# Modulation's vector products in runs of four weight units, most of them moved into the second block's first layer

## The chip, the cores and the metric

One core of one Trainium2 chip. The metric is the device time of one execution in microseconds (us), the median over several executions. One execution was also taken by the hardware profiler, and all rows below come from that one.

## What is computed

Two blocks of two layers each work on 256 tokens of width 1024. The second block's layers also carry 256 context tokens in layer 0, so that their matrix products have 512 token columns there. What the change touches is the modulation of the second block: three vectors for each of two conditions, from one vector of 1024 times a matrix of 1024 x 3072.

```
def hybrid_layer_2(xs, cs, c, c_ctx, norm_g, w_mod, b_mod, w_in, b_in, ...):
    shift_x, scale_x, gate_x = jnp.split(jax.nn.silu(c) @ w_mod + b_mod, 3, axis=-1)
    shift_c, scale_c, gate_c = jnp.split(jax.nn.silu(c_ctx) @ w_mod + b_mod, 3, axis=-1)
    hx = rms_norm(xs, norm_g) * (1 + scale_x[:, None]) + shift_x[:, None]
    hc = rms_norm(cs, norm_g) * (1 + scale_c) + shift_c
    px = split_cols(hx @ w_in + b_in)
    ...
    xs = xs + gate_x[:, None] * merge(px, ya_x, yb_x, yc_x)
    ...

def reference(...):
    x = first_block(x, w_in, b_f, ...)          # two attention layers
    return second_block(x, c_2, ctx_2, ...)     # two of hybrid_layer_2
```

## The kernel before

All weights pass through one stream, `WStream`. A weight unit is 128 partitions x 1024 floats (512 KB) in most cases. `_dma` (L113 to L123) issues its load on the SP queue into a buffer of the tag `wraw`; there are four of these (`RAW` in `KN`). `_split` (L125 to L136) turns it into two single-pass operands, `wh` by a cast on ACT (L133) and `wl` by a subtraction on DVE (L134), in rings of five buffers (`WB`). When both are done, the `wraw` buffer is free for the next load. The table of units has one order, and loads are issued on SP in that order, each waiting there until its buffer is free. `ahead(i)` (L147) keeps the program's loads six units and its splits three units ahead of unit i.

A product with a split unit is three matmuls for each piece (L163, L164, L165: high x high, low x high, high x low). In the second block's layer 0 a unit's 24 matmuls have 512 columns; in the first block a unit has 12 of them.

The modulation is 48 units, 24 for each layer of the second block. Names: `1mod00` is layer 1, vector 0, eighth 0 of the contraction; vector 1 is the scale, 0 the shift, 2 the gate, and `MORDER` puts them as 1, 0, 2. Such a unit isn't split: `whole` (L138) hands out the raw float buffer, and PE reads it directly in four matmuls of 256 columns, each with a 32-wide stationary operand in its own quarter of the array (L749). A float matmul is two PE instructions in the trace, so that a unit is eight instructions. Its `wraw` buffer is free when its four matmuls are through.

Where the 48 units stand is set by `FILL`: a list of a weight unit's name and a number. `get(key)` of that unit first draws so many modulation units from the generator `mod_stream` (L740), and the table of loads has them directly ahead of that unit. `1B2 2` puts two units ahead of `1B2`, the third unit of product B in the first block's layer 1. In the names, `1A` to `1I` and `1O` are the first block's layer 1; `0AKV`, `0AQ`, `0BQ`, `0Va`, `0Vb`, `0GK`, `0GQ`, `0GV`, `0ag`, `0m3_`, `0oa` are the second block's layer 0, in this order; `1GK`, `1GV`, `1ag` are its layer 1. The scale and the shift of layer 0 are needed by the second block's first normalization, its gate only at that layer's end, and layer 1's at the next normalization. The order in which an engine runs its instructions is fixed when the program is built, by priorities that follow the order in which the code is written.

Of the kernel before, what the change touches and what calls it, by code (L numbers as in the profile page):

```python
# [38 lines left out]

MORDER = (1, 0, 2)  # L40

FILL = '1B2 2 1E2 3 1D2 3 1F0 2 1G0 2 1H2 1 0Va0 2 0Va1 2 0Va2 2 0GV0 1 0ag0 2 0ag2 2 1GV0 3 1ag0 2 1ag2 2 1A0 1 0BQ2 2 1F2 2 1GK0 1 1B0 1 1A3 5 1C2 1 0ag1 1 1H0 1 0GK0 2'

# [55 lines left out]
class WStream:  # L101
# [50 lines left out]

    def get(self, key):
        self.ad, self.asp = self.looks.pop(key, (self.ad, self.asp))
        for _ in range(self.fills.pop(key, 0)):
            next(self.stream)
        i = self.idx[key]
        self.ahead(i)
        return self.spl[i]
# [581 lines left out]
def mod_stream(g, l, W):  # L741

    nc, sp, pp = g.nc, g.sp, g.pp
    for s in MORDER:
        ps = pp.tile([128, 256], F32, name=f'mod{l}{s}', tag='gm', bufs=g.GM)
        for k in range(8):
            w = W.whole(f'{l}mod{s}{k}')
            for q in range(4):
                nc.tensor.matmul(ps[32 * q:32 * q + 32], g.cz[:, k // 2, 2 * (k % 2):2 * (k % 2) + 32],  # L749
                                 w[:, 0, 256 * q:256 * q + 256], start=k == 0, stop=k == 7)  # L750
            if k < 7:
                yield
        r = sp.tile([128, 256], F32, name=f'modr{l}{s}', tag='tg', bufs=TG)
        nc.scalar.copy(r, ps)
        pt = pp.tile([128, 2, 4, 2], F32, name=f'modt{l}{s}', tag='at', bufs=g.AT)
        for i in range(2):
            nc.tensor.matmul(pt[:, i].rearrange("p q w -> p (q w)"), r[:, 128 * i:128 * i + 128], g.sel8,
                             start=True, stop=True)
        ks = slice(8 * s, 8 * s + 8)
        v = lambda t: t.rearrange("p (q i) w -> p q i w", q=4)  # L760
        nc.vector.tensor_add(v(g.mod[l][:, ks, :]), pt.rearrange("p i q w -> p q i w"),
                             v(g.bmod[l][:, ks, None].to_broadcast([128, 8, 2])))
        if s == 1:

            nc.vector.scalar_tensor_tensor(g.modA[l], g.mod[l][:, ks, :], 1.0,
                                           g.ng[l][:, :, None].to_broadcast([128, 8, 2]), op0=OP.add, op1=OP.mult)
        yield
# [915 lines left out]
def program(ctx, tc, ins, out, parts=(1, 2)):  # L1683
# [3 lines left out]
    f32 = {e[0] for e in mods}  # L1687
    fs = FILL.split()
    fills = {k: int(n) for k, n in zip(fs[::2], fs[1::2])}
# [19 lines left out]
    looks = {k: (int(a), int(b)) for k, a, b in zip(ls[::3], ls[1::3], ls[2::3])}  # L1709
    W = WStream(g, tab, looks, f32, fills)  # L1710
    W.stream = itertools.chain(mod_stream(g, 0, W), mod_stream(g, 1, W))

    xsp = g.dram.tile([128, 2048], F32, name='xsp')
# [80 lines left out]
```

## Time and profile before

| what | value |
|---|---|
| median of 3 runs | 1210.46 us (1206.68 to 1213.55) |
| profiled execution, its own time | 1205.08 us |
| its span, first to last instruction | 1203.3 us |
| mean granted clock of TensorE | 0.996 |
| busy: PE, DVE, ACT | 1179.3, 919.3, 571.3 us |
| instructions on L749 (modulation) | 384 PE matmul instructions, 48 units |

Engines: PE is TensorE's matmul, PEld its weight load, DVE VectorE, ACT ScalarE, SP the engine on whose queue the loads are issued (SPq). Busy time of PE is modelled from the starts of pipelined matmuls, so a busy PE can still lose time between them; the distance of two starts says more than the duration. Times in rows are microseconds from the span's start.

### The profile page before, as it was taken

To read this page: it belongs to the slowest core of one execution; us is meant where nothing else is said; L and a number is where in the kernel's file an instruction comes from. 1 tells how busy PE (TensorE), PEld (TensorE's weight loads), DVE (VectorE), ACT (ScalarE), POOL (GpSimd) and SP (SyncE) were. 2 spreads that over 40 slices of the span, in tenths; PEclk is the share of its full clock that TensorE was granted. 3 is DMA by queue.
4 is the path that set the end of the run, shared out by engine and by line. 5 is a ranking of instruction groups with operands and counts; after the bars stand their busy time and mean duration, and the time that the engine had idled before them with its cause. 6 is when DMAs were issued, how large, how long until landed. Compare 5 with 4: busy or idle time off the path is not lost.

```text
span 1203.3 us, 20615 instructions
## 1 busy us (share of the span) xinstructions
PE 1179.3 (98%) x8012; PEld 980.5 (81%) x8012; DVE 919.3 (76%) x2050; ACT 571.3 (47%) x1024; POOL 11.2 (1%) x42
## 2 busy tenths in 40 slices
PE   8999999999999999999899999999999999999998
PEld 6878767677887777777788888888999768999998
DVE  5996766966799769989955535755799887896984
ACT  5556534466565433246354522433455433855552
POOL 0000000000000000000000000000000000000000
PEclk9999999999999999999999999999999999999999
DMA  7734566565555632141032232324545323653552
GB/s 249 227 122 135 184 200 233 162 219 198 187 188 207 197 135 73 43 133 54 19 124 70 88 98 78 105 90 173 176 141 189 108 89 101 198 159 123 176 176 71
DMA packets 48258, 171.33 MB, mean 142 GB/s; under 512 B 5340, under 2 KB 6492, under 8 KB 47392
## 3 DMA queue, kind: packets, MB, share of 16 engines
q1 hardware_dynamic: 48160, 170.01, 43.5%
q8 instruction: 63, 1.03, 0.4%
q14 instruction: 35, 0.29, 0.1%
HBM read 167.89 MB, written 2.10 MB: 141 GB/s over the span
## 4 chain that ended last, share of the span: by engine, by line
PE 75%; DVE 14%; DMA 4%; ACT 4%; issue 2%; SPq 0%; ACTq 0%; DVEq 0%
PE f0m L163 3%; PE f0m L165 3%; PE f0m L164 3%; PE f1m L165 2%; PE f1m L163 2%; PE f1m L164 2%; PE mod L749 1%; PE po L164 1%; PE po L165 1%; PE po L163 1%; PE go L165 1%; PE go L164 1%; PE go L163 1%; PE yog L165 1%; PE yoc L165 1%
## 5 line engine op out<-in xcount | busy, mean ns | idle before, releaser
L991 DVE SCALAR_TENSOR_TENSOR ucv<-up,par,ucv 128x512 f32<-128x512 f32 (+1 forms) x240 | 146.9, 612 | 2.2
L163 PE MATMUL f0m<-hTh,wh_0m 128*128 128x512 f32 x192 | 75.7, 394 | 0.0
L164 PE MATMUL f0m<-hTl,wh_0m 128*128 128x512 f32 x192 | 75.4, 393 | 0.0
L165 PE MATMUL f0m<-hTh,wl_0m 128*128 128x512 f32 x192 | 75.2, 392 | 0.0
L163 PE MATMUL f1m<-hTh,wh_1m 128*128 128x256 f32 x192 | 54.9, 286 | 0.1
L165 PE MATMUL f1m<-hTh,wl_1m 128*128 128x256 f32 x192 | 54.8, 286 | 0.0
L164 PE MATMUL f1m<-hTl,wh_1m 128*128 128x256 f32 x192 | 54.5, 284 | 0.0
L134 DVE TENSOR_TENSOR wl_0m<-wr_0m,wh_0m 128x1024 fp32r<-128x1024 f32 x24 | 29.3, 1221 | 25.5 <-ACT wh_0m L133 25.5
L133 ACT CAST wh_0m<-wr_0m 128x1024 fp32r<-128x1024 f32 x24 | 25.2, 1051 | 43.8 <-PE f0m L164 15.2
L163 PEld LDWEIGHTS f0m<-hTh,wh_0m 128*128 128x128 f32 x192 | 36.3, 189 | 7.7 <-DVE wl_0m L134 0.3
L164 PEld LDWEIGHTS f0m<-hTl,wh_0m 128*128 128x128 f32 x192 | 36.1, 188 | 7.5 <-issue 0.2
L165 PEld LDWEIGHTS f0m<-hTh,wl_0m 128*128 128x128 f32 x192 | 36.2, 189 | 7.3
L163 PEld LDWEIGHTS f1m<-hTh,wh_1m 128*128 128x128 f32 x192 | 36.8, 192 | 0.5 <-ACT wh_1m L133 0.3
L165 PEld LDWEIGHTS f1m<-hTh,wl_1m 128*128 128x128 f32 x192 | 36.7, 191 | 0.2 <-DVE wl_1m L134 0.2
L164 PEld LDWEIGHTS f1m<-hTl,wh_1m 128*128 128x128 f32 x192 | 36.7, 191 | 0.1
L133 ACT CAST wh_1m<-wr_1m 128x1024 fp32r<-128x1024 f32 x24 | 25.0, 1049 | 24.4 <-PE f1m L164 9.9
L134 DVE TENSOR_TENSOR wl_1m<-wr_1m,wh_1m 128x1024 fp32r<-128x1024 f32 x24 | 29.3, 1220 | 8.6 <-ACT wh_1m L133 8.4
L1271 ACT ACTIVATE mtm<-f0m,hbin 128x512 f32<-128x512 f32 x24 | 16.3, 681 | 7.6 <-DVE acc L1284 7.3
L134 DVE TENSOR_TENSOR wl_0o<-wr_0o,wh_0o 128x1024 fp32r<-128x1024 f32 x8 | 9.8, 1224 | 13.2 <-ACT wh_0o L133 13.2
L1385 DVE SCALAR_TENSOR_TENSOR xT<-po,mod,xT 128x256 f32<-128x256 f32 x16 | 7.7, 483 | 14.6 <-PE po L165 14.6
L164 PE MATMUL po<-mgl,wh_0o 128*128 128x256 f32 x64 | 18.2, 285 | 0.0
L164 PE MATMUL pp<-mgl,wh_0p 128*128 128x256 f32 x64 | 18.2, 284 | 0.0
(1854 smaller groups left out, 3979.8 us busy)
## 6 DMA issues: line engine op xcount, KB each, us to landing
wr_0mod<-in_wm_dram SPq DMA_DIRECT2D x24, 512.0 KB, 4.3
wr_1mod<-in_wm_dram SPq DMA_DIRECT2D x24, 512.0 KB, 3.7
wr_0m<-in_w_dram SPq DMA_DIRECT2D x24, 512.0 KB, 3.5
wr_1m<-in_w_dram SPq DMA_DIRECT2D x24, 512.0 KB, 3.5
wr_0O<-in_w1o_dram SPq DMA_DIRECT2D x8, 512.0 KB, 3.6
wr_1O<-in_w1o_dram SPq DMA_DIRECT2D x8, 512.0 KB, 3.5
wr_0o<-in_wo_dram SPq DMA_DIRECT2D x8, 512.0 KB, 3.5
wr_0p<-in_wo_dram SPq DMA_DIRECT2D x8, 512.0 KB, 4.3
```

The lines of the kernel that those rows point to most:

```text
L133: g.nc.scalar.copy(wh, r)
L134: g.nc.vector.tensor_sub(wl, r, wh.bitcast(F32))
L163: nc.tensor.matmul(out, lh, rh, start=start, stop=False)
L164: nc.tensor.matmul(out, lh, rl, start=False, stop=False)
L165: nc.tensor.matmul(out, ll, rh, start=False, stop=stop)
L749: nc.tensor.matmul(ps[32 * q:32 * q + 32], g.cz[:, k // 2, 2 * (k % 2):2 * (k % 2) + 32], w[:, 0, 256 * q:256 * q + 256], start=k == 0, st ...
L991: yield nc.vector.scalar_tensor_tensor(o, src, dw[:, i, j:j + 1], o, op0=OP.mult, op1=OP.add)
L1271: nc.scalar.activation(sg, pm, AF.Tanh, scale=0.5, bias=hb[:, blk(n, f)])
L1385: nc.vector.scalar_tensor_tensor(r[:, f, :], ps[:, :256], g.mod[l][:, 16 + f, w:w + 1], r[:, f, :], op0=OP.mult, op1=OP.add)
```

## The change

`FILL` is another list. Of the 48 modulation units, 24 stood in the first block's layer 1, 16 in the second block's layer 0 and 8 in its layer 1; now 16 stand in the first block's layer 1 (as 1, 5, 1, 2, 3 and 4) and 32 in the second block's layer 0 (eight times 4). `get` now cuts a number into runs of at most four units. At the first unit of a run of more than one, `mod_stream` issues the loads of the whole run, and the run's first matmul waits for the last load of the run as well.

```
-FILL = '1B2 2 1E2 3 1D2 3 1F0 2 1G0 2 1H2 1 0Va0 2 0Va1 2 0Va2 2 0GV0 1 0ag0 2 0ag2 2 1GV0 3 1ag0 2 1ag2 2 1A0 1 0BQ2 2 1F2 2 1GK0 1 1B0 1 1A3 5 1C2 1 0ag1 1 1H0 1 0GK0 2'
+FILL = '1A0 1 1A3 5 1B0 1 1B2 2 1E2 3 1D2 4 0Va0 4 0Va1 4 0Va3 4 0GK0 4 0GV0 4 0ag0 4 0ag3 4 0m3_2 4'
...
-        for _ in range(self.fills.pop(key, 0)):
+        n = self.fills.pop(key, 0)
+        for j in range(n):
+
+            self.go = min(4, n - j) if j % 4 == 0 else 0
             next(self.stream)
...
+            i = W.idx[f'{l}mod{s}{k}']
+            if W.go > 1:
+                W.ahead(i + W.go - 1)
+                last = W.loads[W.table[i + W.go - 1][0]]
             w = W.whole(f'{l}mod{s}{k}')
             for q in range(4):
-                nc.tensor.matmul(ps[32 * q:32 * q + 32], g.cz[:, k // 2, 2 * (k % 2):2 * (k % 2) + 32],
+                m = nc.tensor.matmul(ps[32 * q:32 * q + 32], g.cz[:, k // 2, 2 * (k % 2):2 * (k % 2) + 32],
                                  w[:, 0, 256 * q:256 * q + 256], start=k == 0, stop=k == 7)
+                if W.go > 1 and q == 0:
+                    g.wait(m, last)
```

PE, second block, from the last product of `0BQ` to the first of `0Va0`. Before (`t0BQ` and `f0Va` are the products' accumulators, `wh`/`wl` the split weights, `wr_1mod12` a raw modulation unit):

```order
L163 MATMUL t0BQ3_4149<-wh_0BQ3_4173,hTh1_0_3339 128x512
L749 MATMUL mod11_4170<-wr_1mod12_4150,cz_1338 32x256 x4
L749 MATMUL mod11_4170<-wr_1mod13_4158,cz_1338 32x256 x4
L163 MATMUL f0Va0_4303<-hTh0_0_3338,wh_0Va0_4197 128x512
L164 MATMUL f0Va0_4303<-hTl0_0_3340,wh_0Va0_4197 128x512
L164 MATMUL t0BQ2_4148<-wl_0BQ3_4174,hTh1_0_3339 128x512
```

The same place in the change:

```order
L168 MATMUL t0BQ3_4098<-wh_0BQ3_4101,hTl1_0_3286 128x512
L756 MATMUL mod02_4213<-wr_0mod20_3887,cz_1338 32x256
L940 MATMUL akt02_4027<-cst_66,kb2_0_3995 128x128
L926 MATMUL lrt03_4062<-cst_66,kb3_0_4058 96x128
L756 MATMUL mod02_4213<-wr_0mod20_3887,cz_1338 32x256 x3
L756 MATMUL mod02_4213<-wr_0mod21_3899,cz_1338 32x256 x4
L756 MATMUL mod02_4213<-wr_0mod22_4099,cz_1338 32x256 x4
L756 MATMUL mod02_4213<-wr_0mod23_4111,cz_1338 32x256 x4
L940 MATMUL akt03_4090<-cst_66,kb3_0_4058 128x128
L166 MATMUL f0Va0_4248<-hTh0_0_3283,wh_0Va0_4222 128x512
L167 MATMUL f0Va0_4248<-hTl0_0_3285,wh_0Va0_4222 128x512
L166 MATMUL f0Vb0_4275<-hTh0_0_3283,wh_0Vb0_4226 128x512
```

Two units in a run have become four, and `0BQ3`'s remaining products, which stood behind the run, now stand ahead of it.

SP, the loads around the same place, with the semaphores that each waits for. Before:

```order
L120 DMA wr_1mod12_4150<-in_wm_1_dram 128x1024 [waits DMAHW0_49,PE_49]
L120 DMA wr_1mod13_4158<-in_wm_1_dram 128x1024 [waits DMAHW1_49,PE_49]
L120 DMA wr_0Va0_4171<-in_w2_0_dram 128x1024 [waits DMAHW3_49,DVE_49]
L120 DMA wr_0Vb0_4181<-in_w2_0_dram 128x1024 [waits DMAHW5_49,PE_49]
L120 DMA wr_1mod14_4187<-in_wm_1_dram 128x1024 [waits DMAHW6_49,PE_49]
```

In the change:

```order
L120 DMA wr_0mod20_3887<-in_wm_0_dram 128x1024 [waits DMAHW3_49,DMAHW6_49,DVE_49,Activation_49]
L120 DMA wr_0mod21_3899<-in_wm_0_dram 128x1024 [waits DMAHW7_49,DMAHW4_49,DVE_49]
L120 DMA wr_0mod22_4099<-in_wm_0_dram 128x1024 [waits DMAHW0_49,DVE_49]
L120 DMA wr_0mod23_4111<-in_wm_0_dram 128x1024 [waits DMAHW1_49,DVE_49,Activation_49]
L871 DMA gvb_0_3696<-in_rowp_dram 128x512 [waits DVE_49]
L120 DMA wr_0Va0_4119<-in_w2_0_dram 128x1024 [waits DMAHW3_49,PE_49]
L120 DMA wr_0Vb0_4127<-in_w2_0_dram 128x1024 [waits DMAHW4_49,PE_49]
```

`0Va0`'s load waited for a split on DVE and now waits for PE; with four units in a row in the table, the four buffers ahead of it are all the run's own.

PE, the run ahead of `0ag3`, in the change alone (before, no unit stood here):

```order
L756 MATMUL mod12_5814<-wr_1mod23_5712,cz_1338 32x256 x4
L166 MATMUL f0ag3_5857<-hTh0_0_3283,wh_0ag3_5823 128x512
L167 MATMUL f0ag3_5857<-hTl0_0_3285,wh_0ag3_5823 128x512
L166 MATMUL f0m3_0_5891<-hTh0_0_3283,wh_0m3_0_5827 128x512
L167 MATMUL f0m3_0_5891<-hTl0_0_3285,wh_0m3_0_5827 128x512
L166 MATMUL f0m3_1_5920<-hTh0_0_3283,wh_0m3_1_5831 128x512
L168 MATMUL f0ag3_5857<-hTh0_0_3283,wl_0ag3_5824 128x512
```

Behind the run come at once the first products of three units that stand behind it in the table of loads.

## Rows read from the trace of the kernel before

**Rows 1.** The page: the span; PE's busy time, share and instructions.

```profile
span 1203.3 us, 20615 instructions
PE 1179.3 (98%) x8012; PEld 980.5 (81%) x8012; DVE 919.3 (76%) x2050; ACT 571.3 (47%) x1024; POOL 11.2 (1%) x42
```

**Rows 2.** Waits of PE over the span (total us, times, longest).

```profile
PE mod L749 <- DMA wr_0mod<-in_wm_dram: 1.1, 1, 1.1
PE f0Va L163 <- ACT wh_0Va L133: 0.8, 1, 0.8
```

**Rows 3.** Timeline of PE, first modulation runs (start, us, engine, line, op, out<-in, count).

```profile
163.21 0.62 PE L749 MATMUL mod<-wr_0mod,cz 128*32 128x256 f32 x4
...
165.08 0.66 PE L636 MATMUL yt<-cst,mx 128*128 128x128 f32 x4
165.49 0.46 PE L163 MATMUL g1A<-wh_1A,xTh 128*128 128x460 f32 x1
165.78 0.37 PE L164 MATMUL g1A<-wl_1A,xTh 128*128 128x460 f32 x1
166.09 0.64 PE L749 MATMUL mod<-wr_0mod,cz 128*32 128x256 f32 x8
166.66 0.48 PE L165 MATMUL g1A<-wh_1A,xTl 128*128 128x460 f32 x1
166.97 0.37 PE L163 MATMUL g1A<-wh_1A,xTh 128*128 128x460 f32 x1
167.18 0.37 PE L164 MATMUL g1A<-wl_1A,xTh 128*128 128x460 f32 x1
```

**Rows 4.** Timeline of PE, last modulation run of the kernel.

```profile
1016.65 0.28 PE L164 MATMUL f1ag<-hTl,wh_1ag 128*128 128x256 f32 x1
1016.77 0.28 PE L165 MATMUL f1ag<-hTh,wl_1ag 128*128 128x256 f32 x1
1016.98 1.07 PE L749 MATMUL mod<-wr_1mod,cz 128*32 128x256 f32 x16
1017.98 0.39 PE L163 MATMUL f1ag<-hTh,wh_1ag 128*128 128x256 f32 x1
1018.20 0.28 PE L164 MATMUL f1ag<-hTl,wh_1ag 128*128 128x256 f32 x1
```

**Rows 5.** Timeline of PE around the run of three units ahead of `1E2`, and `1E3`.

```profile
202.69 0.39 PE L164 MATMUL g1E<-wl_1E,xTh 128*128 128x512 f32 x1
202.92 0.39 PE L165 MATMUL g1E<-wh_1E,xTl 128*128 128x512 f32 x1
203.24 1.50 PE L749 MATMUL mod<-wr_0mod,cz 128*32 128x256 f32 x24
204.67 0.50 PE L163 MATMUL g1E<-wh_1E,xTh 128*128 128x512 f32 x1
...
208.62 0.73 PE L163 MATMUL g1E<-wh_1E,xTh 128*128 128x512 f32 x2
...
209.93 0.50 PE L164 MATMUL g1E<-wl_1E,xTh 128*128 128x512 f32 x1
```

**Rows 6.** Timeline of SP's queue: the issue of `1E3`'s load.

```profile
203.94 0.33 SPq L120 DMA_DIRECT2D wr_1E<-in_w_dram  x1
```

**Rows 7.** Timeline of ACT: the cast of `1E3`, with ACT's idle time before it.

```profile
207.53 1.05 ACT L133 CAST wh_1E<-wr_1E 128x1024 fp32r<-128x1024 f32 x1 [3.64 <-DMA wr_1E<-in_w_dram]
```

**Rows 8.** Timeline of ACT: casts of two loads that landed one behind the other.

```profile
408.11 1.05 ACT L133 CAST wh_0Vb<-wr_0Vb 128x1024 fp32r<-128x1024 f32 x1 [1.95 <-DMA wr_0Vb<-in_w_dram]
409.49 1.05 ACT L133 CAST wh_0Va<-wr_0Va 128x1024 fp32r<-128x1024 f32 x1 [0.33 <-DMA wr_0Va<-in_w_dram]
```

**Rows 9.** The four loads of tile `wr_0Va`, from issue to landing.

```profile
DMA to landing us min/median/max: 4.4/5.0/5.5
```

**Rows 10.** Busy time by stretch: us, PE, PEld, DVE, ACT, POOL, PEclk, DMA share, GB/s.

```profile
596.00:600.40 4.40, 2.10 (x39) 1.57 (x38) 4.40 (x11) 0.00 (x0) 0.17 (x2) 1.00 0.00 0
600.40:607.20 6.80, 6.80 (x42) 5.92 (x40) 6.80 (x9) 0.69 (x1) 0.00 (x0) 0.52 0.49 134
```

## The prediction

> **What bounds the kernel now.** I read the page first, then the timeline of PE around L749, then the queues of the loads. The page gives PE 1179.3 of the span's 1203.3 us [rows 1]: there is no stage in which another engine has the time to spare that PE lacks, so what counts is how far apart PE's matmuls start. The list of PE's waits shows how little it stands still for weights in the steady part: its longest wait for a load is 1.1 us in one place, and 0.8 us in one place for a cast [rows 2]. So the change can win only what PE pays for the modulation itself, and it can lose whatever it opens between PE's matmuls.
>
> **What a run costs.** The timeline shows 36 separate runs of L749, from 163.21 to 1016.98 [rows 3, 4]. Around the run of 8 instructions the matmul before starts at 165.78 and the second one after at 166.97; without the run these two steps would take 0.21 each (166.97 to 167.18), so the run costs 1.19 - 0.42 = 0.77 us [rows 3]. Around the run of 16 it is 1.43 - 2 x 0.12 = 1.19 us [rows 4]. Eight more instructions cost 0.42, and a run has a fixed price of 0.35 us. The matmuls in a run overlap in the array; entering and leaving the narrow stationary shape is what costs.
>
> **Term 1, fewer runs.** In the order of the change PE has 20 runs instead of 36: nine in the first block (transposes still cut some), eleven in the second, because the run ahead of `0ag0` stands in three pieces and the one ahead of `0Va0` in two. That saves 16 x 0.35 = 5.6 us. The number of products is the same, so nothing else of the modulation's own time moves. The waits of 1.1 and 0.8 us [rows 2] lie in runs that are regrouped; I count both as gone. Together 7.5 us gained.
>
> **Term 2, the load behind a run.** There are four `wraw` buffers, and loads are issued in the table's order. With four modulation units in a row, all four hold the run's own units until PE has gone through them. The unit that stands behind the run can begin to load only when the run's first unit is through; before, a run of at most three left it a buffer. The order of SP shows it: `0Va0`'s load now waits for PE. No weight is prefetched over a run of four any more.
>
> The price of that chain stands in the trace, where other work covered it. The run of three ahead of `1E2` starts at 203.24 [rows 5]. The unit whose load has to wait for that run's first unit is `1E3`, four places on: its load is issued at 203.94 [rows 6], its cast begins at 207.53 when the load has landed [rows 7], and its first matmul starts at 208.62 [rows 5]. That is 5.38 us from the run's start. Then `1E2`'s products hid it. A run of 24 instructions lets the next matmul start after 204.67 - 203.24 = 1.43 us [rows 5]; one of 32 needs 0.42 more, 1.85 us. So PE stands for 5.38 - 1.85 = 3.5 us behind each run of four, less what the order puts there that needs no new weight.
>
> Two things lengthen it. Two loads that land one behind the other are 1.38 us apart at their casts [rows 8], and in several places the order has the second unit's first products right behind two of the first unit's (0.46 us at 0.23 each [rows 5]): 0.9 us more. Where a unit's low part comes at once, its first product starts at 209.93, that is 1.31 us after the first one with the high part [rows 5], with two products of 0.23 between: 0.85 more.
>
> For the cover I price by starts: 0.23 for 512 columns [rows 5], 0.12 for 256 [rows 4], 0.10 for a transpose (four in 165.08 to 165.49 [rows 3]), and 0.05 for a narrow product, like an instruction of a run. By place, cover first, then what remains with the lengthening:
>
> - `0Va0`: a transpose, 0.1; remains 4.3 (second unit).
> - `0Va1`: four transposes, seven score products, two small ones, 1.4; remains 3.0 (second unit).
> - `0Va3`: transposes, scores and eight narrow products, 2.1; remains 2.1 (second unit, partly covered).
> - `0GK0`: two transposes, four scores, 0.7; remains 3.7 (low part).
> - `0GV0`: 0.7; remains 2.8.
> - `0ag0`: the run's three pieces with scores between; remains 2.0 for the third unit.
> - `0ag3`: nothing; 3.5 and, since the second and the third unit come at once, 1.8: 5.3.
> - `0m3_2`: two gate products, four cumulative ones, 1.0; remains 3.4 (low part).
> - `1D2` in the first block: transposes, scores and two wide products, 1.6; remains 3.0 (its low part is the second product).
> - `1A3`: the run waits for its fourth load; a wait stood there before, so I take 0.7.
>
> The sum is 30.3 us of new waits. Nothing covers them later: PE is the bound on either side. Waiting for a run's own last load I cost at nothing: in the second block its buffer comes free with a split, which runs ahead, and eight or more products of 0.23 stand between; if DVE is late with that split, each of the eight runs waits up to the landing, some 3.6 us (203.94 to 207.53).
>
> The bounds: with the landing of [rows 7] and no lengthening, ten chains less their cover are about 21 us. With landings of 5.0 us, the median of `wr_0Va`'s four loads [rows 9], in place of 3.6, each is 1.4 longer and the sum about 44. I take the middle, since a load behind a run finds the queue empty, as `1E3`'s did.
>
> **Term 3, the clock.** A stretch of 4.4 us in which PE was busy 2.10 us was followed by 6.8 us at a granted clock of 0.52, the lower of its two levels (1.2 GHz of 2.4), while PE was busy all the time [rows 10]; that costs 6.8 x 0.48 = 3.3 us. Waits of 3.5 us and more are of this kind, waits of 1.1 us were not. Four places are at 3.4 or above; I take three drops, 10 us. Nothing bounds it but none (0) and all ten (33).
>
> The Trainium skill, "TensorE: Matmul & The Clock Gate", section "HAM oscillation — how this bites in real kernels", describes a kernel that loses its clock in every round because it waits for the next slice of weights between bursts of matmuls. [...]
>
> **Sum.** 30.3 + 10 - 7.5 = 33 us on the profiled execution's 1205.08, 1238 us. The median shown is 1210.46, 5.4 above it; on that basis 1243, rounded to 1242.
>
> **The moves themselves.** Eight units fewer in the first block relieve its loads, but PE waited there for almost none [rows 2], so I take nothing. Layer 1 of the second block loses its eight units and eight of the 36 runs, which are in term 1. The gate of layer 0 and all of layer 1 come in time: the last run stands ahead of `0m3_2`, long before the layer's end.
>
> **The rivals.**
>
> *Every wait loses the clock.* Ten drops instead of three: 1210.5 + 30.3 + 33 - 7.5 = 1266. For it: the stretch of [rows 10] had 2.3 us without matmul, and six of my waits are longer than that. Against: some are 2 to 3 us with dense products on both sides. Chance 0.17. In the skill's section the drop is the rule; here one stretch shows it.
>
> *Attention's products cover the waits, and only term 1 is left: faster.* 1210.5 - 7.5 = 1203. The place is behind the runs at `0Va1`, `0Va3`, `0GV0` and `0ag0`, where the order has put scores and transposes. It decides at 3.5 us of cover for a run. Against: I count 0.1 to 2.1 us, and at `0Va0` and `0ag3` next to none. Chance 0.06.
>
> *The change doesn't do what it says.* The order already cuts two of the eight runs; if the loads of the first unit behind a run land early by the same token, waits shrink to about what term 1 gains: within 6 us of 1210. Chance 0.06.
>
> **How the numbers follow.** The forecast, 1222 to 1257 with its bounds, has 0.71; the clock rival reaches to 1268 and beyond. The range 1220 to 1268 holds the forecast and most of that rival, about 8 in 10. A measurement of this kernel tells about 0.5% (6 us) from no change. Faster by more than that 0.06, within it 0.06, slower 0.88.
>
> **What would show it.** In the profile after: about 20 runs of L749, in all some 6 us cheaper; between 370 and 620 us eight gaps of PE behind them of 2 to 5 us, put down to `wh_0Va`, `wh_0GK`, `wh_0GV`, `wh_0ag`, `wh_0m` on ACT or to their loads; loads issued 0.7 us after a run's start and landing 3.6 later; stretches of the low clock behind the longest. The first block and layer 1 of the second should be the same or a few us shorter. I am wrong if these gaps are below 1 us, if PE stands ahead of the runs (for their own last load) rather than behind them, or if the clock stays up.

## The result, and the profile after

The changed kernel takes 1240.62 us, the median of 4 runs (1238.17 to 1244.30), beside 1209.36 (1206.68 to 1213.55, 4 runs) for the kernel before in the same session: a ratio of 1.0277, with a 95% interval of 1.0251 to 1.0303. It is slower by some 31 to 33 us. The profiled execution took 1238.17 us, at a mean granted clock of 0.984 (before 0.996).

From the page of the changed kernel, the span and PE, and the granted clock in 40 slices:

```profile
span 1236.4 us, 20644 instructions
...
PE 1182.9 (96%) x8012; PEld 986.6 (80%) x8012; DVE 921.8 (75%) x2050; ACT 572.6 (46%) x1024; POOL 11.2 (1%) x42
...
PEclk9999999999997999999999999999999999999999
```

The span grew by 33.1 us, and PE's busy time by only 3.6 [rows 1]. To see where, both spans are cut at the same two matmuls: the last product of `0BQ` and the first of `yoa`. The middle stretch holds all the places of the second block's layer 0 at which the change puts its runs, but the last one. Busy time by stretch (us, PE, PEld, DVE, ACT, POOL with counts, PEclk, DMA share, GB/s), the changed kernel:

```profile
0.00:378.49 378.49, 362.76 (x2196) 289.55 (x2197) 303.11 (x809) 207.28 (x436) 4.17 (x20) 0.99 0.54 180
378.49:600.43 221.94, 197.82 (x1322) 146.19 (x1321) 170.96 (x307) 70.53 (x110) 3.42 (x9) 0.95 0.37 124
600.43:1236.40 635.97, 622.36 (x4497) 550.89 (x4495) 447.70 (x935) 294.76 (x479) 3.61 (x13) 0.99 0.37 119
```

And the kernel before, cut at the same matmuls:

```profile
0.00:384.88 384.88, 371.90 (x2298) 291.93 (x2299) 301.66 (x799) 208.39 (x437) 4.16 (x20) 1.00 0.57 191
384.88:565.89 181.01, 179.94 (x1189) 137.38 (x1188) 153.22 (x291) 74.89 (x116) 3.24 (x7) 1.00 0.35 113
565.89:1203.30 637.41, 627.47 (x4527) 551.17 (x4525) 464.40 (x962) 288.01 (x472) 3.76 (x15) 0.99 0.38 121
```

The first stretch is 6.4 us shorter, the last 1.4, and the middle 40.9 longer: -6.4 + 40.9 - 1.4 = 33.1. In the middle PE stood idle for 221.94 - 197.82 = 24.1 us, where it was 1.1: that is 23.0 us of waits. The other 17.9 us of the middle are busy time: the sixteen more units that now lie there, 16 x 0.42 = 6.7 by [rows 3, 4], and products at the lower clock.

PE's longest waits in the changed kernel (us in total, times, longest), without one at the kernel's very start that stands in both, against the two of [rows 2]:

```profile
PE f0Va L168 <- DVE wl_0Va L134: 4.9, 1, 4.9
PE gl000cum L1135 <- DVE la L1128: 4.6, 1, 4.6
PE akt L940 <- DVE kb L907: 4.4, 3, 3.1
PE f0ag L166 <- ACT wh_0ag L133: 3.9, 3, 3.5
PE t0BQ L167 <- DVE wl_0BQ L134: 2.6, 1, 2.6
PE at020mt L1041 <- DVE at020ms L1039: 2.0, 1, 2.0
PE f0GK L166 <- ACT wh_0GK L133: 1.6, 1, 1.6
```

Of the two waits of [rows 2], 1.1 and 0.8 us, 0.6 and 0.5 us are left under the same names, and seven rows of 1.6 us or more have come. One of them is the predicted chain step by step. The timeline behind the run ahead of `0ag3` (start, us, engine, line, op, out<-in, count; in brackets the idle time ahead and what ended it):

```profile
575.74 1.93 PE L756 MATMUL mod<-wr_1mod,cz 128*32 128x256 f32 x32
...
576.44 0.33 SPq L120 DMA_DIRECT2D wr_0ag<-in_w_dram  x1
...
580.02 1.04 ACT L133 CAST wh_0ag<-wr_0ag 128x1024 fp32r<-128x1024 f32 x1 [1.53 <-DMA wr_0ag<-in_w_dram]
...
581.12 0.50 PE L166 MATMUL f0ag<-hTh,wh_0ag 128*128 128x512 f32 x1 [3.45 <-ACT wh_0ag L133]
```

The load is issued 0.70 us after the run's start, the cast begins 3.58 later, and the first product 1.10 after that: 5.38 us in all, as in [rows 5 to 7], and PE stands for 3.45.

The same chain stands behind the other runs, though the list of waits puts most of its time down to something else, because attention's products lie in between. Two examples, the runs ahead of `0GK0` and `0GV0`, each with the first product of the unit behind it:

```profile
453.56 1.93 PE L756 MATMUL mod<-wr_1mod,cz 128*32 128x256 f32 x32
...
458.85 0.50 PE L166 MATMUL f0GK<-hTh,wh_0GK 128*128 128x512 f32 x1 [1.63 <-ACT wh_0GK L133]
...
497.26 1.93 PE L756 MATMUL mod<-wr_1mod,cz 128*32 128x256 f32 x32
...
502.60 0.74 PE L166 MATMUL t0GV<-wh_0GV,hTh 128*128 128x512 f32 x2 [0.51 <-ACT wh_0GV L133]
```

From the run's start to that product these are 5.29 and 5.34 us; in them PE stands idle for 2.4 and 2.5 us.

The costliest place is another, the run ahead of `0Va0`. The same view there:

```profile
375.04 0.33 SPq L120 DMA_DIRECT2D wr_0mod<-in_wm_dram  x1
...
379.73 1.93 PE L756 MATMUL mod<-wr_0mod,cz 128*32 128x256 f32 x30
...
380.42 0.33 SPq L120 DMA_DIRECT2D wr_0Va<-in_w_dram  x1
...
384.65 1.05 ACT L133 CAST wh_0Va<-wr_0Va 128x1024 fp32r<-128x1024 f32 x1
...
392.61 1.21 DVE L134 TENSOR_TENSOR wl_0Va<-wr_0Va,wh_0Va 128x1024 fp32r<-128x1024 f32 x1
...
393.87 0.79 PE L168 MATMUL f0Va<-hTh,wl_0Va 128*128 128x512 f32 x1 [4.91 <-DVE wl_0Va L134]
```

The run's fourth unit begins to load at 375.04 only, when `0BQ`'s last split is done; the run stands behind it, `0Va0`'s load behind the run, and the low part of `0Va0` on DVE comes 8 us after its cast on ACT, behind attention's norms, which the program has put ahead of it. The run's first piece, two instructions, stands at 378.82. From the last product of `0BQ` (378.49) to the next run (406.13) all this takes 27.6 us.

### The profile page after: what moved, and what is told of

It reads as the page before. It is cut to its first block, busy times and chain, and to the rows that moved or that the text cites. A ratio compares the mean times of both kernels' runs of the same rounds, so it can differ in the third digit from the quotient of the medians.

```text
span 1236.4 us, 20644 instructions
## 1 busy us (share of the span) xinstructions
PE 1182.9 (96%) x8012; PEld 986.6 (80%) x8012; DVE 921.8 (75%) x2050; ACT 572.6 (46%) x1024; POOL 11.2 (1%) x42
## 4 chain that ended last, share of the span: by engine, by line
PE 63%; DVE 8%; ACT 4%; DMA 1%; issue 1%; ACTq 0%; SPq 0%
PE f0m L166 3%; PE f0m L168 3%; PE f0m L167 3%; PE f1m L167 2%; PE f1m L166 2%; PE f1m L168 2%; PE po L167 1%; PE po L168 1%; PE po L166 1%; PE yoc L166 1%; PE yog L167 1%; PE yog L166 1%; PE yoc L168 1%; PE yoc L167 1%; PE yog L168 1%
## 5 line engine op out<-in xcount | busy, mean ns | idle before, releaser
L133 ACT CAST wh_0m<-wr_0m 128x1024 fp32r<-128x1024 f32 x24 | 25.1, 1050 | 40.9 <-PE f0m L167 15.6
L133 ACT CAST wh_1m<-wr_1m 128x1024 fp32r<-128x1024 f32 x24 | 25.0, 1048 | 24.1 <-PE f1m L167 9.2
L988 DVE SCALAR_TENSOR_TENSOR up<-vt,up 128x512 f32<-128x512 f32 (+1 forms) x8 | 4.5, 558 | 28.7 <-ACT vt L985 28.7
L1293 DVE SCALAR_TENSOR_TENSOR acc<-mtm,yoa 128x512 f32<-128x512 f32 x8 | 5.5, 686 | 23.6 <-PE yoa L168 23.6
L168 PE MATMUL f0Va<-hTh,wl_0Va 128*128 128x512 f32 x32 | 14.0, 438 | 4.9 <-DVE wl_0Va L134 4.9
```

What stands on the lines that cost most here:

```text
L133: g.nc.scalar.copy(wh, r)
L168: nc.tensor.matmul(out, ll, rh, start=False, stop=stop)
L988: nc.vector.scalar_tensor_tensor(mid, tg.rearrange("p (s t) -> p s t", t=256), 1.0, mid, op0=OP.add, op1=OP.mult)
L1293: last = nc.vector.scalar_tensor_tensor(a, sg[mb], 1.0, py[:, :NT], op0=OP.add, op1=OP.mult)
```

## The experiments

The theory is that of the prediction: a run of four holds all four `wraw` buffers, so no weight is loaded over it. Its rivals in what follows are the place (attention's dense part is a bad place for any run), and the added wait of a run's first product for its last load. All ratios are against runs of the kernel before on the same chip (medians 1205.48 to 1206.55 us). On that basis the changed kernel is 1239 to 1240 us.

**Three units a run instead of four.** The same 16 units stay in the first block, and the same 32 in layer 0.

```diff
-FILL = '... 1D2 4 0Va0 4 0Va1 4 0Va3 4 0GK0 4 0GV0 4 0ag0 4 0ag3 4 0m3_2 4'
+FILL = '... 1D2 4 0Va0 3 0Va1 3 0Va3 3 0GK0 3 0GQ0 3 0GV0 3 0GV2 2 0ag0 3 0ag3 3 0m3_2 3 0m3_4 3'
```

> The change with the second block's 32 units in ten runs of three and one of two instead of eight runs of four; the first block as in the change. Buffers theory (four raw buffers, all held by a run of four, so that the unit behind it starts to load only when the run is half through): one buffer is left for the unit behind a run, so the gaps of 2 to 5 us behind the runs mostly go and the time falls by 15 to 30 us, to 1211 to 1226 us. Place theory (32 units in the second block's layer 0 are too many, whatever the length of a run): within 6 us of 1240 us.

Measured: 1200.00 us (1197.86 to 1201.75), ratio 0.9950 [0.9935, 0.9966]. That is 40 us below the changed kernel, and faster than the kernel before. Its middle stretch, in the same view and cut at the same matmuls:

```profile
380.49:571.04 190.55, 188.86 (x1282) 140.96 (x1280) 154.01 (x290) 70.15 (x111) 3.24 (x7) 1.00 0.41 136
```

PE is idle there for 1.7 us instead of 24.1, at the full clock. The same work at the same layer costs nothing, so the place is not the cause. The theory expected less of it than came.

**One run of four in the kernel before.** The two units ahead of `0ag2`, the one ahead of `0ag1` and one of the two ahead of `0ag0` are gathered in one run of four. The rest of the program is the changed one, so that the added wait for the last load stands here too, ahead of this run and of the kernel's other runs of more than one unit.

```diff
-... 0ag0 2 0ag2 2 ... 0ag1 1 ...
+... 0ag0 1 0ag3 4 ...
```

> The list of before, with the two units ahead of 0ag2, the one ahead of 0ag1 and one of the two ahead of 0ag0 joined into one run of four ahead of 0ag3; nothing else. Buffers theory: one wait of 4 to 6 us behind this run, with or without 3.3 us of low clock, less 0.35 us for each run saved: 3 to 9 us slower than before. Place theory: the units stay in the same layer, so within 2 us of before.

Measured: 1209.58 us (1208.35 to 1213.75), ratio 1.0036 [1.0014, 1.0058], 3 to 4 us more. On PE the run stands as three units (536.36) and one (538.63), with three of attention's products between. Behind it is a gap of 2.75 us, which the profile puts down to attention's `at031ms` on DVE. The load's chain ends there as well: the load behind the run is issued at 537.06, 0.70 us after the run's start, its cast on ACT runs from 540.92 to 541.97, `at031ms` is done at 541.98, and the product starts at 542.02. So the gap fits the theory as the time does. It doesn't prove it: the two ends can't be told apart, and the 3 to 4 us also hold a wait of 5.0 us for `yag` ahead of a product of `yoa`, which the kernel before doesn't have.

**The first run later.** Its units stand ahead of `0Va2` instead of `0Va0`.

```diff
-... 0Va0 4 0Va1 4 0Va3 4 ...
+... 0Va1 4 0Va2 4 0Va3 4 ...
```

> The change with the second block's first run of four moved from ahead of 0Va0 to ahead of 0Va2. Buffers theory alone: a wait of about 4 us goes and another of about 3 us comes, 1236 to 1241 us. DVE theory (between 342 and 394 us DVE is busy nearly all the time with the keys' and queries' norms, and the run ahead of 0Va0 takes from PE the only products that need nothing of DVE): the place alone costs about 13 us more than another, so 1223 to 1231 us.

Measured: 1233.81 us (1230.15 to 1235.75), ratio 1.0236 [1.0208, 1.0265], 5 to 6 us less than the changed kernel and between the two forecasts. `0Va1`'s run becomes the first, and behind it PE stands for 3.27 us for `wh_0Va`.

**Without the wait for the last load.** The runs stay at four in the list, but each unit's products go when that unit has landed.

```diff
-                if W.go > 1 and q == 0:
-                    g.wait(m, last)
```

> The change without the run's first product waiting for the run's last load; each product still waits for its own load. Buffers theory: PE waits behind the runs and not ahead of them, so within 4 us of 1240 us. Rival (the added wait is what costs): below 1225 us, and PE no longer idle behind the runs.

Measured: 1217.77 us (1215.28 to 1220.61), ratio 1.0108 [1.0078, 1.0138]. The wait is worth 20 us by the ratios and 22 by the medians. The theory's forecast failed here. The rival's time held; its second half, PE no longer idle behind the runs, did not. The trace shows how the two hang together. At `0Va0`:

```profile
373.49 1.50 PE L756 MATMUL mod<-wr_0mod,cz 128*32 128x256 f32 x24
...
374.62 0.37 SPq L120 DMA_DIRECT2D wr_0Va<-in_w_dram  x1
...
378.61 0.64 PE L756 MATMUL mod<-wr_0mod,cz 128*32 128x256 f32 x8
...
379.67 1.03 ACT L133 CAST wh_0Va<-wr_0Va 128x1024 fp32r<-128x1024 f32 x1
...
380.73 1.23 DVE L134 TENSOR_TENSOR wl_0Va<-wr_0Va,wh_0Va 128x1024 fp32r<-128x1024 f32 x1
```

Without the wait the run falls apart into three units and one. The three go 6.2 us earlier (379.73 to 373.49), `0Va0`'s load 5.8 earlier, and DVE splits it 11.9 us earlier (392.61 to 380.73), ahead of attention's norms. The run ahead of `0ag3` breaks up too, and its gap of 3.45 us is gone. The other runs of the second block stayed as they were, and a loss stayed with them: by the view of the stretches, PE is still idle for 206.08 - 194.03 = 12.1 us of the middle one.

```profile
378.29:584.37 206.08, 194.03 (x1298) 144.68 (x1297) 171.90 (x313) 70.18 (x110) 3.41 (x9) 0.97 0.39 131
```

So the wait does harm by gathering four units at the moment when they hold all buffers; the next runs test that.

**Two more load buffers, and its control.** The sizes of the rings are set in one line; the room for two more `wraw` buffers comes from one less of `wh` and of `wl`. The control gives up the same split buffers for nothing.

```diff
-KN = (5, 3, 4, 5, 2, 12, 6, 5, 2, 4)
+KN = (5, 3, 6, 4, 2, 12, 6, 5, 2, 4)
```

The control has `4, 4` in place of `6, 4`.

> The changed kernel with six buffers for loads in place of four; the room comes from one buffer less of the split high and low parts each (four in place of five). Theory of the buffers: a run of four now leaves two buffers for the weights behind it, so their loads are issued before the run, PE's 23 us of idle time between 378 and 600 us shrink below 6, and the time falls to 1198 to 1214 us. Rival, the place and the added wait (which holds PE's products and DVE's order whatever the buffers): as the next kernel, 1230 or more.

> The control of the run before: the changed kernel with four buffers for loads as it has, and the same loss of one split buffer. Theory of the buffers: the wait stays, 1232 to 1255 us; the distance to the run before, 20 us or more, is what two load buffers are worth. Rival: both within 6 us of each other.

Measured: 1200.06 us (1198.14 to 1203.29), ratio 0.9954 [0.9940, 0.9969], against 1245.55 (1245.26 to 1246.07), ratio 1.0330 [1.0314, 1.0345] for the control. Both forecasts of the theory held. Two load buffers are worth 45 us with the change's list, runs of four and added wait untouched. How, the run ahead of `0Va1` shows:

```profile
383.16 0.38 SPq L120 DMA_DIRECT2D wr_0Va<-in_w_dram  x1
...
390.16 1.05 ACT L133 CAST wh_0Va<-wr_0Va 128x1024 fp32r<-128x1024 f32 x1
...
391.98 1.93 PE L756 MATMUL mod<-wr_0mod,cz 128*32 128x256 f32 x32
393.84 0.50 PE L166 MATMUL f0Va<-hTh,wh_0Va 128*128 128x512 f32 x1
```

The weight behind the run is issued 8.8 us ahead of it and cast before it starts; the next product begins 1.86 us after the run's start, which is the run's own length in the prediction (1.85).

**Runs of three without the wait.** The same edit as above, on the kernel of threes.

```diff
-                if W.go > 1 and q == 0:
-                    g.wait(m, last)
```

> Runs of three as in the first run of this study, without the wait of each run's first product for its last load. Theory of the buffers: with three units a run leaves a buffer in any case, so the wait costs nothing: within 5 us of the kernel of threes (1195 to 1205). Rival, the wait itself costs, as its removal gave 23 us in the runs of four: 1190 or less.

Measured: 1202.72 us (1201.60 to 1205.34), ratio 0.9975 [0.9964, 0.9986]. With a buffer left over the wait costs nothing; it may even help by some 3 us (the two intervals just touch).

**Runs of two.** The layer's 32 units in sixteen groups of two; in the first block the four ahead of `1D2` are two groups of two as well.

```diff
-FILL = '... 1D2 4 0Va0 3 0Va1 3 0Va3 3 0GK0 3 ...'
+FILL = '... 1D2 2 1D3 2 0BQ2 2 0Va0 2 0Va1 2 0Va2 2 0Va3 2 0GK0 2 0GK1 2 0GV0 2 0GV2 2 0ag0 2 0ag1 2 0ag2 2 0ag3 2 0m3_0 2 0m3_2 2 0m3_4 2'
```

> The same units at the same layer, but the second block's in runs of two. By the fixed price of a run: 33 runs in place of the 27 of the kernel of threes, 6 x 0.35 = 2.1 us more, two buffers left over in each: 1199 to 1206 us. Rival, one buffer left over is still too few and a second one gains: below 1196.

Measured: 1200.83 us (1200.69 to 1203.46), ratio 0.9960 [0.9946, 0.9974], not to be told from the threes.

**Only the first run shorter.** Three units ahead of `0Va0`, the fourth put behind the last run; all other runs stay at four.

```diff
-... 0Va0 4 ... 0m3_2 4'
+... 0Va0 3 ... 0m3_2 4 0m3_4 1'
```

> The changed kernel with one unit less in its first run of the second block (three ahead of 0Va0 in place of four; the unit goes behind the last run, ahead of 0m3_4). By the trace of the changed kernel the stretch from 0BQ's last product to the next run lost 16 us at this place; theory that the fourth unit there holds the whole chain up (its load waits for the last split of 0BQ, the run stands behind it, 0Va's loads behind the run, and DVE's order puts 0Va's low parts behind attention's): 12 to 18 us less, 1222 to 1229. Rival, the price of the prediction for this place, 4.3 us and one drop of the clock of 3.3: 1232 to 1238.

Measured: 1231.89 us (1227.60 to 1233.77), ratio 1.0207 [1.0180, 1.0233], 8 us less, between the two forecasts and 0.1 us from the rival's. At the place itself the theory held: from the last product of `0BQ` to the next run it is 14.2 us (380.51 to 394.72) instead of 27.6, so 13.4 less. The run of three now stands ahead of that product (375.72), so that the run's own time lies outside the 14.2 but inside the 27.6. From the run ahead of `1D2` to the one ahead of `0Va1`, which both kernels have, it is 156.5 us (238.22 to 394.72) instead of 171.2 (234.91 to 406.13), 14.7 less. But part was given back, for behind that next run a wait stands open that attention had covered before:

```profile
394.72 1.93 PE L756 MATMUL mod<-wr_0mod,cz 128*32 128x256 f32 x32
...
395.42 0.35 SPq L120 DMA_DIRECT2D wr_0Va<-in_w_dram  x1
...
398.96 1.04 ACT L133 CAST wh_0Va<-wr_0Va 128x1024 fp32r<-128x1024 f32 x1 [2.91 <-DMA wr_0Va<-in_w_dram]
...
400.05 0.79 PE L166 MATMUL f0Va<-hTh,wh_0Va 128*128 128x512 f32 x1 [3.40 <-ACT wh_0Va L133]
```

The program's order is made anew by every edit, so the prices of single places needn't add up.

**One more load buffer.** `KN` with `5, 4` in place of `4, 5`: a run of four leaves one.

```diff
-KN = (5, 3, 4, 5, 2, 12, 6, 5, 2, 4)
+KN = (5, 3, 5, 4, 2, 12, 6, 5, 2, 4)
```

> The changed kernel with five load buffers (and four split ones), so that a run of four leaves one. Theory of the buffers: one left is enough, as in the runs of three: 1197 to 1208 us. Rival: what counts is two left, or the place of the first run: 1215 or more.

Measured: 1200.11 us (1197.64 to 1200.94), ratio 0.9942 [0.9923, 0.9962]. One buffer left over is as good as two.

**The kernel before, and the threes, with six load buffers.** Both with `KN` of the run with two more.

> The kernel before, with its own list and no added wait, with six load buffers and four split ones. Theory: it hardly waits for loads, so the buffers give nothing and the split ones cost a little: within 4 us of the kernel before; the 0.5% that the changed kernel gains with six buffers is then the moves' and the fewer runs'. Rival: the buffers alone give it: ratio below 0.996.

> Runs of three with six load buffers and four split ones, the two remedies together. Theory: either one alone has removed the waits, so together they give no more: 1196 to 1202 us. Rival: three buffers left over gain again: below 1194.

Measured: the kernel before with six buffers 1203.28 us (1201.32 to 1205.20), ratio 0.9973 [0.9960, 0.9987]: 3 us less, within the 4 of the forecast. Its interval lies below 1, so the buffers alone give this kernel a little too, and of the 0.5% that the changed list reaches with them only 0.2% is left for the moves and the fewer runs. The threes with six buffers: 1197.26 us (1194.41 to 1197.89), ratio 0.9921 [0.9902, 0.9940], the fastest kernel of this study, and better than the kernel before with the same buffers. Their forecast held.

## Why the prediction was right

The forecast of 1242 us met 1240.6. Its cause is shown, too: the same list with one buffer more, or with runs one unit shorter, loses nothing. That the two figures lie so near is in part luck, since errors in single terms cancelled. Step by step:

- **Term 1, fewer runs** (7.5 us gained). The 20 runs came. Of the two waits, 1.9 us, 1.1 are left; 0.6 of them stand ahead of `1A3`, where term 2 had priced 0.7. The price of a run fits, but isn't shown: with six buffers the kernel before has 31 runs and the changed one 24, 7 x 0.35 = 2.5 us, and their ratios, 0.9973 and 0.9954, are 0.2% apart, 2.3 us, but the two intervals overlap and the moves lie in that difference too.
- **Term 2, the load behind a run** (30.3 us). The mechanism held, and so did the sum: 23.0 us of waits in the middle stretch, and the 4.6 behind the last run, which stands outside it, make 27.6. The chain of 5.38 us came to the hundredth at `0ag3`. At the other runs of four from `1D2` on, the first product of the unit behind starts 5.3 to 6.0 us after the run's start too (`0Va0` and `0ag0` counted from their second pieces); only at `0m3_2` it takes 9.9. What the prediction had wrong is what covers that time. PE's idle time from the run to that product, with the price in brackets: `0Va0` 3.6 (4.3), `0Va1` 1.5 (3.0), `0Va3` 0.9 (2.1), `0GK0` 2.4 (3.7), `0GV0` 2.5 (2.8), `0ag0` 0 (2.0), `0ag3` 3.5 (5.3), `0m3_2` 5.1 (3.4), `1D2` in the first block 0.8 (3.0). That is 20.3 us where 29.6 were priced. The other waits of the middle stretch, most of them for next units and low parts as the prices include them, add 4.8, and 4.9 more come from a wait that had no price: `0Va0`'s low part, late by DVE's order. So the sum was met by luck in part. The 4.6 behind `0m3_2` are put down to the gate's chain (`la`) instead of `wh_0m`, whose cast stands behind that chain's work on ACT; with the first run of three the same hole reads 3.3 us for `wh_0m`.
- **"Waiting for a run's own last load I cost at nothing."** This step failed. PE hardly stands ahead of the runs, as forecast, but the order of the program waits: it puts the whole run behind the last load, and with it the release of all four buffers. Taking that wait out gave 20 to 22 us, which the sum had booked under term 2 as if it came with the length of the run alone.
- **Term 3, the clock** (10 us for three drops). Six stretches at the lower level came, 34.1 us together, where the kernel before has the 6.8 of [rows 10] (both without the kernel's start and end). The two longest, in the view of the stretches:

```profile
384.30:398.00 13.70, 7.02 (x15) 4.44 (x16) 11.79 (x42) 5.04 (x9) 0.00 (x0) 0.51 0.51 176
...
613.00:619.90 6.90, 5.83 (x18) 4.95 (x19) 6.50 (x8) 6.87 (x10) 0.00 (x0) 0.53 0.47 143
```

  The longest covers a wait: PE is busy for 7.02 of 13.7 us, so by half of its busy time it costs some 3.5 us. In the middle stretch, where four of the six lie, the busy time beyond the kernel before is 17.9 us. The kernel of threes, at full clock, has 188.86 - 179.94 = 8.9 for eleven units and more runs; five further units at 0.42 make 11.0, and 6.9 remain for the clock. By the units alone (6.7) it would be 11.2. PE's busy time in the four is 16.2 us, and half of it 8, so 7 to 8 us is the better estimate; in the other two it is 8.3, half 4. Some 11 to 12 us for all six, then: the term is near, with twice the drops at less than the price of 3.3 each, and that is luck again.
- **The moves at nothing.** The first stretch gained 6.4 us, though the wait of 2.6 us for `wl_0BQ` lies in it; the last gained 1.4, though the 4.6 behind the last run lie in it. That is more than "a few" in either, but the units' own time in the middle, the 6.7 us above, stands against it, and so do the fewer runs of term 1. (Layer 1 of the second block lost seven runs, not eight.) What the moves alone are worth isn't shown; the 2.3 us between the two lists with six buffers, runs included, speak for little.
- **The rivals.** Of the rule of the Trainium skill, "TensorE: Matmul & The Clock Gate", section "HAM oscillation — how this bites in real kernels", by which a kernel that waits for its next operands between bursts of matmuls loses its clock in every round, the trace shows half. Five of the six drops came some 5 to 7 us after the start of one of the ten runs, and the other five runs had none. By the list of waits only three of the six came in or behind a wait for a weight (`t0BQ`, `f0GK`, `f0ag`). All six cost some 12 us and not the 33 of the rival by which every wait loses the clock, since part of their time PE stood anyway. "Attention covers the waits" was true at `0ag0`, more than half true at `0Va1` and `0Va3`, and nowhere near the whole. (Seven, not six, of the priced waits are longer than the 2.3 us that the clock rival is measured by.)

What stays open: how the 13 to 15 us at `0Va0` divide between the late load, DVE's order and the clock, and what the 0.3% of the kernel before with six buffers are made of.

## What to carry to other kernels

Before operands are gathered in a longer run, count the load buffers: a run that takes as many as the ring has stops every load behind it, and each time lays bare as much of that load's chain as other products don't cover (here 5.4 us less the run's own length at `0ag3`, nothing at `0ag0`). One buffer left over removed all of it here. A wait that gathers a group at its last load made it worse, as it also delays the group's release: 20 to 22 us with a full ring, nothing with one buffer left. Price such places with the order of the other engines too: at the costliest one the late split stood behind other work in DVE's fixed order.

## What the runs showed of the hardware

The lower clock came at shorter waits than I had thought. Ahead of the drop just behind 459.4 us of the changed kernel PE's longest gap was 1.6 us, and ahead of that just behind 411.7 none was above 0.7 us; the stretches before them:

```profile
408.00:411.70 3.70, 2.17 (x18) 1.69 (x15) 0.86 (x2) 2.05 (x4) 0.00 (x0) 1.00 0.90 348
455.00:459.40 4.40, 1.96 (x20) 1.01 (x10) 3.83 (x8) 2.69 (x5) 0.00 (x0) 1.00 0.93 330
```

PE was at work in about half of either, with many small attention products. So a loose stretch without a single long wait was followed by the lower level as well; I had tied it to waits of 3.5 us. In the profiled executions of the kernels of threes and of pairs the lower level didn't come between the kernel's start and its end: a mean granted clock of 1.000.
